# A hybrid mLSTM and attention block on one core: the later modulation sections summed on GpSimd during attention, and the inverse row sums spread by DMA

## The chip, the cores and the metric

The kernel runs on one core of a Trainium2 chip. A core has five engines with a queue of instructions each: TensorE (PE, matmuls; its weight loads are shown apart as PEld), VectorE (DVE), ScalarE (ACT), GpSimd (POOL) and SyncE (SP, which issues nearly all DMA transfers here). The metric is the device time of one launch in microseconds (us); less is better.

## The reference, cut to what matters

One layer of width 1024 on 1024 tokens with 256 tokens of context. A vector `c` gives six sections of 1024 numbers each, which shift, scale and gate the two halves of the layer:

```python
mod = (silu(c) @ w_mod + b_mod)                  # [1024] x [1024, 6*1024]
sh1, sc1, g1, sh2, sc2, g2 = split(mod, 6)
h = rmsnorm(x, norm1_g) * (1 + sc1) + sh1        # the context likewise, from c_ctx
y = token_mix(h, hc, ...)                        # input projections, mLSTM, attention, w_pa, w_pb, w_o
x = x + g1 * y
x = x + g2 * swiglu(rmsnorm(x, norm2_g) * (1 + sc2) + sh2, w_ffn_gate, w_ffn_up, w_ffn_down)
return rmsnorm(x, final_g)
```

Attention has 8 heads of width 128 with 2 key/value heads, over the 1024 tokens and the 256 of the context. Sections 0 and 1 are needed before the first projection. Section 2 (g1) is needed when `w_o` is loaded, which is scaled by it; sections 3 and 4 with the second norm; section 5 (g2) at the down projection.

## The kernel before, in words

Everything is in 32-bit floats. A product is made of three matmuls (`mm3`, L104 to L106) of operands split into a high and a low part (`split`, L98 on ACT and L99 on GpSimd or DVE). The stages follow one another: input projections in units of `w_in` (to about 800 us), mLSTM heads (to 1050), the merge of the mLSTM's halves, attention (about 1079 to 1393), a loop over eight column blocks n of `w_pb` (to 1506), a loop over `w_o` (to 1600), gate and up projections (to 2070) and the down projection. The Tile framework takes the program in the order in which it is written, sets the waits, and moves instructions within each engine's queue; an engine runs its queue strictly in order, so a waiting instruction holds all that stand behind it.

**Modulation.** `modulation_rest` computes half a section (512 columns) at each call and is called eight times: behind units 14 and 15 of the `w_in` loop, behind n = 1, 2, 4 and 5 of the `w_pb` loop, and behind u = 1 and 2 of the `w_o` loop. These are called places 0 to 7 below. A place loads four pieces of `w_mod` of 512 KB on SP (L293), runs 8 matmuls over them into one bank of PSUM (L300; the profile has 16 records for them), copies the bank to SBUF on DVE (L304), and then runs either one matmul that sums the four partial rows (L344, for the gates of sections 2 and 5) or four matmuls that also turn the row into a column (L312, for sections 3 and 4). L344 and L312 wait for the copy L304, and stand in PE's queue between the projection's matmuls.

**Attention** runs 64 steps (2 groups of heads, 8 blocks of 128 tokens, 4 heads). Four steps make a block; blocks are numbered 0 to 15 here. A step computes scores (L104 to L106 into `sc`), maxima (L1033), exponentials on ACT (L1043), the sum and its reciprocal (L1044, L1045), which DVE puts into a column of a tile `dg`, the transposes (L1054) and their split (L1057, L1058). `dg` is cleared by GpSimd ahead of each block (L1100). `attn_values` then multiplies by the values, for all four heads of the block before, in four parts spread over the next block's steps. In part 1 PE transposes `dg` (L1071), DVE copies the result (L1073), and GpSimd spreads the four rows of inverse sums over the 128 partitions with four `partition_broadcast`s (L1076) into `rs`. Behind part 3 DVE multiplies by `rs` (L1080). The next block's tokens are loaded by SP as `qr` (L1016). SP's queue during attention holds these loads and a few of keys, values and weights.

Of the kernel before, what the change touches and what calls it, by code (L numbers as in the profile page):

```python
# [9 lines left out]
F32 = mybir.dt.float32  # L10
F32R = mybir.dt.float32r
AF = mybir.ActivationFunctionType
ALU = mybir.AluOpType
# [4 lines left out]
P = 128  # L18
D = 1024
KT = D // P  # L20
S = 1024
CT = 256
NT = S // P
# [64 lines left out]
class Block:  # L88
# [241 lines left out]
                    nc.vector.tensor_tensor(t, v, bm[:, 8 + k:10 + k], op=ALU.add)  # L330
                    nc.vector.scalar_tensor_tensor(out=self.A1[:, s, k:k + 2], in0=t, scalar=1.0, in1=g1[:, k:k + 2], op0=ALU.add, op1=ALU.mult)

    def modulation_rest(self, ps, i):

        nc = self.nc
        bm = self.ch("b_mod")
        j0, b = (2, 5, 3, 4)[i // 2], i % 2
        c0 = j0 * D + b * 512
        rows = self.mod_block(ps, "X", (c0, c0 + 256))
        if i < 4:  # L340
            row = self.slots.get([P, 1024], F32)
            nc.sync.dma_start(row[0:1, 0:512], self.io["b_mod"][0:1, c0:c0 + 512])
            o = ps("Y", "mg")
            nc.tensor.matmul(o[0:2, :], lhsT=self.sel, rhs=rows[:, 0], start=True, stop=True)  # L344
            nc.vector.tensor_tensor(row[0:1, 512:1024], o[0:1, :], row[0:1, 0:512], op=ALU.add)
            nc.sync.dma_start(self.d_g[i // 2:i // 2 + 1, b * 512:(b + 1) * 512], row[0:1, 512:1024])
            self.slots.put(rows, row)
            return
        m = self.mod_channels(rows, ps, "Y", 1)[:, :, 0]
        hs = slice(4 * b, 4 * b + 4)  # L350
        if j0 == 3:
            nc.vector.tensor_tensor(self.B2[:, hs], m, bm[:, 24 + 4 * b:28 + 4 * b], op=ALU.add)
        else:
            t = self.st.tile([P, 4], F32, name="modt2", tag="modt2", bufs=2)
            nc.vector.tensor_tensor(t, m, bm[:, 32 + 4 * b:36 + 4 * b], op=ALU.add)
            nc.vector.scalar_tensor_tensor(out=self.A2[:, hs], in0=t, scalar=1.0, in1=self.ch("norm2_g")[:, hs], op0=ALU.add, op1=ALU.mult)


    def first_loads(self):
# [700 lines left out]
    def attn_values(self, pool, ps, g, t, PT, vv, dg, ya, part):  # L1060

        nc = self.nc
        if part == 0:
            self.av = ps("Z", "av")
        av = self.av
        for s in ((0, 1, 2), (3, 4), (5, 6, 7), (8, 9))[part]:
            pt = PT[s // 4]
            self.mm3(av, (vv[0][:, s], vv[1][:, s]), (pt[0][:, s % 4], pt[1][:, s % 4]), s == 0, s == NP - 1)
        if part == 1:
            rb = ps("Y", "pt")  # L1070
            nc.tensor.transpose(rb[:, 0:P], dg, self.idf)  # L1071
            rows = pool.tile([P, P], F32, name="rrow", tag="rrow", bufs=1)
            nc.vector.tensor_copy(rows, rb[:, 0:P])  # L1073
            self.rs = pool.tile([P, 512], F32, name="rs", tag="rs", bufs=1)
            for h in range(4):
                nc.gpsimd.partition_broadcast(self.rs[:, h * P:(h + 1) * P], rows[32 * h:32 * h + 1, :])  # L1076
        if part < 3:
            return
        rs = self.rs
        nc.vector.tensor_tensor(ya[:, 4 * g:4 * g + 4, t * P:(t + 1) * P], av.rearrange("p (h t) -> p h t", h=4),  # L1080
                                rs.rearrange("p (h t) -> p h t", h=4), op=ALU.mult)

    def attention(self, pool, ps):


        nc = self.nc
        kv, qs, dgs = {}, {}, {}
        kv[0] = self.attn_group_kv(pool, ps, 0)
        qs[0, 0] = self.attn_q(pool, ps, 0, 0)
        steps = [(g, t, h) for g in range(2) for t in range(NT) for h in range(4)]  # L1090

        def scores(i):
            if i >= len(steps):
                return None
            g, t, h = steps[i]
# [12 lines left out]
        yield  # L1108
        pr = scores(0)()
        ptp, ya = yield  # L1110
        PT, pend = None, None
        for i, (g, t, h) in enumerate(steps):
            if g == 0 and t == NT - 2 and h == 0:
                kv[1] = self.attn_group_kv(pool, ps, 1)
            if h and pend:
                self.attn_values(*pend, h)
            nxt = scores(i + 1)
            if h == 0:
                if pend:
                    self.attn_values(*pend, h)  # L1120
                PT = new_pt()
            self.attn_transpose(ps, h, pr, PT)
            if h == 1 and i + 3 < len(steps):
                qs[steps[i + 3][:2]] = self.attn_q(pool, ps, *steps[i + 3][:2])
            if h == 3:
                pend = (pool, ps, g, t, PT, kv[g][1], dgs[g, t], ya)
            pr = nxt() if nxt else None
        for part in range(4):
            self.attn_values(*pend, part)
        yield  # L1130


    def run(self):
        nc, tc, io = self.nc, self.tc, self.io
# [8 lines left out]
        def scratch(name, shape):  # L1143
            return dr.tile(shape, F32, name=name)
# [12 lines left out]
        self.d_mm = scratch("d_mm", [D, S])  # L1157
        self.d_ms = scratch("d_ms", [D, S])
        self.d_x1 = scratch("d_x1", [S, D])
        self.d_act = scratch("d_act", [FT // 2, 7, P, 512])  # L1160

        self.const, close_const = pool("const")
# [87 lines left out]
        X, later = {}, []  # L1250
# [5 lines left out]
        for i, u in enumerate(units):  # L1256
# [20 lines left out]
                more()  # L1277
            if i == 13:
                slots.put(*[t for p in self.cT for t in p])
            if i in (14, 15):  # L1280
                self.modulation_rest(PS, i - 14)
            if i == 22:
                while later:
                    more()
# [63 lines left out]

        pt, close_pt = pool("pt")
        w_pb = [self.load_s(slots, io["w_pb"], 0, KT, n * P, P) for n in range(2)]  # L1350
        attn.send((pt, yaf))
        close_pt()
        close_pa()

# [22 lines left out]
        for n in range(KT):  # L1377
# [15 lines left out]
                self.split(hi[:, n % 2], lo[:, n % 2], t[:, 0])  # L1393
                slots.put(t)
            slots.put(*w)
            if n in (1, 2, 4, 5):
                self.modulation_rest(PS, 3 + n if n < 3 else 2 + n)
            if n == KT - 2:
                load_o(0)
        for half in range(2):  # L1400
# [84 lines left out]
        for i, (half, u) in enumerate(units):  # L1485
# [22 lines left out]
                    r0 = (4 * half + t) * P  # L1508
                    nc.sync.dma_start(self.d_x1[r0:r0 + P, :], x1[t])
            slots.put(*w[0], *w[1])  # L1510
            if not half and u in (1, 2):
                self.modulation_rest(PS, 1 + u)
            if half and u == 2:
                for v in us:
                    self.t_own(v)
# [329 lines left out]
```

## Time and profile before

| | |
|---|---|
| runs of the kernel | 2314.78, 2306.33, 2312.02 us; median 2312.02 |
| the profiled execution | 2319.12 us (its span 2317.3) |
| mean granted TensorE clock | 0.975 |
| PE busy, of the span | 2173.9 us, 94% |
| DVE busy | 1588.6 us, 69% |
| ACT busy | 996.3 us, 43% |
| POOL busy | 767.0 us, 33% |
| DMA, mean rate | 113 GB/s |

Instruction rows of the timeline give a start, a duration, the line and operation, and in brackets the idle time ahead of the instruction with what ended it. Matmuls overlap: the pace of the projections is read from the starts, 0.23 us from one matmul of 512 columns to the next and 0.12 us for 256 columns. The granted clock is a share of full speed: 1.00 is the 2.4 GHz level and 0.50 the 1.2 GHz level.

### The profile page before, as it was taken

The numbers are of one execution on the slowest core, as the hardware profiler recorded it, in microseconds if no ns is written. First come the engines' busy times: TensorE is split into PE (matmuls) and PEld (weight loads), VectorE is DVE, ScalarE is ACT, GpSimd is POOL, SyncE is SP. The second block draws the span as 40 slices with busy tenths as digits, with TensorE's granted clock in tenths as the row PEclk, the third lists the DMA queues.
The fourth block names the chain that finished last, engine by engine and source line by source line (L and its number), as shares of the span: only waits on it lengthen the run. The fifth ranks groups of instructions, "written<-read, shape, count | busy, mean of one in ns | idle before, by whom it ended". The sixth has DMA issues, their size and how long they took to land. (4 is left out here: it accounts for less than half of the span.)

```text
span 2317.3 us, 31157 instructions
## 1 busy us (share of the span) xinstructions
PE 2173.9 (94%) x11387; PEld 1798.3 (78%) x11387; DVE 1588.6 (69%) x2855; ACT 996.3 (43%) x1997; POOL 767.0 (33%) x619
## 2 busy tenths in 40 slices
PE   5899999999999698999999998999899999998997
PEld 2698888977888587877888886789688888876875
DVE  4767576576878786876888873365746464678997
ACT  4424435243443564643777672134523232334332
POOL 1322222312323141311001004331564545457765
PEclk8999999999999899999999999999899999999999
DMA  7132323243232913036000016661132323264421
GB/s 259 55 92 89 103 92 105 83 150 128 70 113 98 310 58 114 13 130 234 15 21 21 15 42 203 220 225 71 46 128 91 118 93 113 97 219 177 159 91 73
DMA packets 179577, 262.43 MB, mean 113 GB/s; under 512 B 13136, under 2 KB 119640, under 8 KB 179424
## 3 DMA queue, kind: packets, MB, share of 16 engines
q1 hardware_dynamic: 169504, 236.62, 30.9%
q10 hardware_dynamic: 9920, 23.82, 2.6%
q8 instruction: 90, 1.47, 0.3%
q14 instruction: 63, 0.52, 0.1%
HBM read 190.10 MB, written 70.30 MB: 112 GB/s over the span
## 5 line engine op out<-in xcount | busy, mean ns | idle before, releaser
L98 ACT ACTIVATE s<-s 128x1024 fp32r<-128x1024 f32 (+2 forms) x446 | 369.5, 851 | 677.4 <-DVE s L233 79.1
L104 PE MATMUL pr<-s,s 128*128 128x512 f32 (+1 forms) x1736 | 624.3, 361 | 19.3 <-DVE s L261 9.9
L106 PE MATMUL pr<-s,s 128*128 128x512 f32 (+1 forms) x1736 | 622.8, 360 | 7.8 <-POOL s L99 4.8
L105 PE MATMUL pr<-s,s 128*128 128x512 f32 (+1 forms) x1736 | 623.4, 360 | 6.9 <-POOL s L99 4.9
L99 POOL TENSOR_TENSOR s<-s,s 128x1024 fp32r<-128x1024 f32 (+1 forms) x199 | 407.9, 2060 | 664.5 <-ACT s L98 455.3
L99 DVE TENSOR_TENSOR s<-s,s 128x1024 fp32r<-128x1024 f32 (+2 forms) x247 | 311.9, 1270 | 128.9 <-ACT s L98 105.5
L104 PEld LDWEIGHTS pr<-s,s 128*128 128x128 f32 x1736 | 331.4, 191 | 76.8 <-ACT s L98 13.1
L106 PEld LDWEIGHTS pr<-s,s 128*128 128x128 f32 x1736 | 330.8, 191 | 62.5 <-POOL s L99 7.0
L105 PEld LDWEIGHTS pr<-s,s 128*128 128x128 f32 x1736 | 331.0, 191 | 57.1 <-POOL s L99 6.0
L104 PE MATMUL pj<-s,s 128*128 128x512 f32 (+1 forms) x696 | 250.9, 361 | 18.1 <-DVE s L1743 13.5
L105 PE MATMUL pj<-s,s 128*128 128x512 f32 (+1 forms) x696 | 247.7, 356 | 7.3 <-POOL s L99 7.3
L106 PE MATMUL pj<-s,s 128*128 128x512 f32 (+1 forms) x696 | 247.5, 356 | 2.3 <-POOL s L99 2.3
L261 DVE TENSOR_TENSOR s<-s,pr 128x512 f32<-128x512 f32 x200 | 133.1, 681 | 84.3 <-PE pr L106 80.0
L1533 DVE TENSOR_TENSOR s<-s,pr 128x512 f32<-128x512 f32 x154 | 100.2, 680 | 114.8 <-ACT s L1549 78.5
L104 PEld LDWEIGHTS pj<-s,s 128*128 128x128 f32 x696 | 133.3, 192 | 50.8 <-DVE s L1743 20.1
L105 PEld LDWEIGHTS pj<-s,s 128*128 128x128 f32 x696 | 133.5, 192 | 25.8 <-POOL s L99 7.7
L106 PEld LDWEIGHTS pj<-s,s 128*128 128x128 f32 x696 | 133.2, 191 | 23.3 <-POOL s L99 3.0
L1058 DVE TENSOR_TENSOR PT<-pt,PT 128x512 fp32r<-128x512 f32 (+1 forms) x192 | 112.5, 598 | 35.3 <-ACT PT L1057 33.1
L1043 ACT ACTIVATE pr<-sc,st 128x512 f32<-128x512 f32 (+1 forms) x192 | 118.2, 623 | 34.4 <-DVE st L1035 33.9
L1543 POOL TENSOR_TENSOR s<-s,s 128x512 f32<-128x512 f32 x44 | 70.3, 1598 | 168.3 <-ACT s L98 71.6
L1057 ACT ACTIVATE PT<-pt 128x512 fp32r<-128x512 f32 (+1 forms) x192 | 94.6, 525 | 55.9 <-PE pt L1054 55.6
L1033 DVE TENSOR_REDUCE st<-sc 128x1 f32<-128x512 f32 (+1 forms) x192 | 109.6, 591 | 0.8 <-PE sc L106 0.8
(313 smaller groups left out, 3528.0 us busy)
## 6 DMA issues: line engine op xcount, KB each, us to landing
s<-in_w_in_dram SPq DMA_DIRECT2D x60, 512.0 KB, 3.7
d_act<-s SPq DMA_DIRECT2D x74, 256.0 KB, 2.1
s<-d_act SPq DMA_DIRECT2D x37, 512.0 KB, 5.3
s<-in_w_mod_dram SPq DMA_DIRECT2D x32, 512.0 KB, 6.1
s<-in_w_ffn_gate_dram SPq DMA_DIRECT2D x22, 512.0 KB, 4.5
s<-in_w_ffn_up_dram SPq DMA_DIRECT2D x22, 512.0 KB, 3.9
s<-in_w_ffn_down_dram SPq DMA_DIRECT2D x22, 512.0 KB, 5.1
s<-in_w_mod_dram SPq DMA_DIRECT2D x32, 256.0 KB, 4.5
```

What stands on the lines that cost most here:

```text
L98: nc.scalar.activation(hi, src, AF.Copy)
L99: (lo_eng or nc.gpsimd).tensor_tensor(lo, src, hi.bitcast(F32), op=ALU.subtract)
L104: nc.tensor.matmul(out, lhsT=lhs[0], rhs=rhs[0], start=first, stop=False)
L105: nc.tensor.matmul(out, lhsT=lhs[0], rhs=rhs[1], start=False, stop=False)
L106: nc.tensor.matmul(out, lhsT=lhs[1], rhs=rhs[0], start=False, stop=last)
L261: eng.tensor_tensor(out, a, b, op=ALU.add)
L1033: nc.vector.tensor_reduce(st[:, j:j + 1], o[:, 0:n], axis=AX.X, op=ALU.max)
L1043: nc.scalar.activation(pr[:, s0:s0 + n], sc[j][:, 0:n], AF.Exp, bias=st[:, 3:4], accum_out=st[:, 4 + j:5 + j])
L1057: nc.scalar.activation(hi, src, AF.Copy)
L1058: nc.vector.tensor_tensor(lo, src, hi.bitcast(F32), op=ALU.subtract)
L1533: nc.vector.tensor_tensor(out, a, b, op=ALU.add)
L1543: nc.gpsimd.tensor_tensor(g, g, o, op=ALU.mult)
```

## The change

`modulation_rest` is now a generator, which attention advances 36 times over its 64 steps: 32 of the advances each take one tile of `w_mod` (128 x 1024, 512 KB, two buffers `wm`, L347 on SP), multiply it on GpSimd by the 128 values of `silu(c)` that belong to its partitions (L362), and add it into an accumulator (L363). Eight such steps make a section. An accumulator is cleared by GpSimd (L352) and takes the row of `b_mod` into its first partition (L353). The other four advances end the sections: two matmuls with a tile of ones (L370), copies (L371) and a store (L372) for sections 2 and 5, or eight matmuls (L376) and one DVE operation for 3 and 4. The eight calls at the places above are gone. In `attn_values` the transpose of `dg` moves from part 1 to part 0, and the four broadcasts become two DMAs on SP: a store of the four rows to DRAM (`d_rs`, L1102) and a load that spreads them over the partitions (`rs`, L1103).

```diff
-    def modulation_rest(self, ps, i):
-        j0, b = (2, 5, 3, 4)[i // 2], i % 2
-        c0 = j0 * D + b * 512
-        rows = self.mod_block(ps, "X", (c0, c0 + 256))
...
+    def modulation_rest(self, pool):
+        nc, slots, ps = self.nc, self.slots, self.ps
+        sections = (2, 3, 4, 5)
+        seq = [(j0, k) for j0 in sections for k in range(KT)]
+        loaded, accs = [], {}
+        def load():
...
+            w = pool.tile([P, D], F32, name="wm", tag="wm", bufs=2)
+            nc.sync.dma_start(w, self.io["w_mod"][k * P:(k + 1) * P, j0 * D:(j0 + 1) * D])
+        def start(j0):
+            accs[j0] = slots.get([P, D], F32)
+            nc.gpsimd.memset(accs[j0], 0.0)
+            nc.sync.dma_start(accs[j0][0:1, :], self.io["b_mod"][0:1, j0 * D:(j0 + 1) * D])
...
+        for i, (j0, k) in enumerate(seq):
+            load()
+            if k == 2 and j0 != sections[-1]:
+                start(j0 + 1)
+            nc.gpsimd.tensor_scalar(loaded[i], loaded[i], self.sc[:, k, 0:1], None, op0=ALU.mult)
+            nc.gpsimd.tensor_tensor(acc, acc, loaded[i], op=ALU.add)
+            yield
+            if k + 1 < KT:
+                continue
+            if j0 in (2, 5):
+                for b in range(2):
+                    o = ps("Y", "mg")
+                    nc.tensor.matmul(o[0:2, :], lhsT=self.ones[:, 0:2], rhs=acc[:, b * 512:(b + 1) * 512], start=True, stop=True)
+                    nc.vector.tensor_copy(acc[0:1, b * 512:(b + 1) * 512], o[0:1, :])
+                nc.sync.dma_start(self.d_g[j0 // 5:j0 // 5 + 1, :], acc[0:1, :])
+            else:
+                m = ps("Y", "mch")
+                for j in range(KT):
+                    nc.tensor.matmul(m[:, j:j + 1], lhsT=acc[:, j * P:(j + 1) * P], rhs=self.ones[:, 0:1], start=True, stop=True)
...
-        if part == 1:
+        if part == 0:
             rb = ps("Y", "pt")
             nc.tensor.transpose(rb[:, 0:P], dg, self.idf)
-            rows = pool.tile([P, P], F32, name="rrow", tag="rrow", bufs=1)
+            rows = pool.tile([P, P], F32, name="rrow", tag="rrow", bufs=2)
             nc.vector.tensor_copy(rows, rb[:, 0:P])
             self.rs = pool.tile([P, 512], F32, name="rs", tag="rs", bufs=1)
-            for h in range(4):
-                nc.gpsimd.partition_broadcast(self.rs[:, h * P:(h + 1) * P], rows[32 * h:32 * h + 1, :])
+            i = g * NT + t
+            nc.sync.dma_start(self.d_rs[i], rows[0:P:32, :])
+            nc.sync.dma_start(self.rs, self.d_rs[i:i + 1].rearrange("o h t -> o (h t)").partition_broadcast(P))
...
+            if (i + 1) * 9 // 16 > i * 9 // 16:
+                next(side, None)
```

Where the scheduler puts the new work is read from the order of the queues. In SP's queue before, the loads of attention's first half follow one another with nothing between them; a last entry x6 stands for six rows alike.

```order
L1000 DMA vr<-d_v 128x2x128
L879 DMA d_ms<-s_9673 128x1024
L129 DMA s_9718<-in_w_pb_dram 128x8x128
L1016 DMA qr<-d_q 128x512 x6
L998 DMA kr<-d_k 128x2x128 x3
```

SP's queue in the change, from the store for block 0 to the loads for block 2 (a row ends with x2 or x4 where that many alike follow each other):

```order
L1102 DMA d_rs<-rrow 4x128
L347 DMA wm<-in_w_mod_dram 128x1024
L1103 DMA rs<-d_rs 128x512
L347 DMA wm<-in_w_mod_dram 128x1024 x2
L1042 DMA qr<-d_q 128x512
L347 DMA wm<-in_w_mod_dram 128x1024 x4
L1102 DMA d_rs<-rrow 4x128
L347 DMA wm<-in_w_mod_dram 128x1024
L1103 DMA rs<-d_rs 128x512
L347 DMA wm<-in_w_mod_dram 128x1024 x2
L1042 DMA qr<-d_q 128x512
L347 DMA wm<-in_w_mod_dram 128x1024 x2
```

Thirteen of the 32 `wm` loads now stand ahead of block 1's store, one more between that store and its load, and 18 in all ahead of block 2's store. From the third on, each `wm` load also waits for GpSimd's step two before it, which frees its buffer.

GpSimd's queue before, over attention's first blocks, behind two splits of weights (the rows named ISA are the broadcasts and what goes with them):

```order
L99 TENSOR_TENSOR s_9714<-s_9712,s_9713 128x1024
L99 TENSOR_TENSOR s_9720<-s_9718,s_9719 128x1024
L1100 MEMSET dg 128x128
L1076 ISA
L1076 ISA rs<-rrow 128x128 x4
L1100 MEMSET dg 128x128
L1076 ISA rs<-rrow 128x128 x4
```

The same queue in the change from the first of these splits on, with the waits in brackets (`s_9779` and `s_10004` are the accumulators of sections 2 and 3):

```order
L99 TENSOR_TENSOR s_9665<-s_9663,s_9664 128x1024 [waits DMAHW0_49,DVE_49,DMAHW4_49,PE_49,Activation_49]
L352 MEMSET s_9779 128x1024 [waits DMAHW5_49,DMAHW6_49,DMAHW1_49,Pool_49]
L362 TENSOR_SCALAR wm<-wm,sc 128x1024 [waits DMAHW3_49,DMAHW1_49]
L362 TENSOR_SCALAR wm<-wm,sc 128x1024 [waits DMAHW7_49,DMAHW4_49]
L363 TENSOR_TENSOR s_9779<-s_9779,wm 128x1024 [waits DMAHW6_49,Pool_49]
L363 TENSOR_TENSOR s_9779<-s_9779,wm 128x1024 [waits Pool_49]
L99 TENSOR_TENSOR s_9671<-s_9669,s_9670 128x1024 [waits DMAHW0_49,PE_49,Activation_49]
L352 MEMSET s_10004 128x1024 [waits DMAHW5_49,DVE_49,Pool_49]
L362 TENSOR_SCALAR wm<-wm,sc 128x1024 [waits DMAHW3_49]
L363 TENSOR_TENSOR s_9779<-s_9779,wm 128x1024 [waits Pool_49]
L362 TENSOR_SCALAR wm<-wm,sc 128x1024 [waits DMAHW5_49]
L363 TENSOR_TENSOR s_9779<-s_9779,wm 128x1024 [waits Pool_49]
```

The broadcasts are gone. Two multiplications and two additions, the first two steps, now stand between the two splits with a clearing ahead of them; behind the second split and another clearing a multiplication and an addition alternate, each multiplication behind the DMA of its tile, and the clearings of `dg` come between them.

## Rows read from the trace of the kernel before

**Rows 1.** The page: PE's busy time, share and instructions.

```profile
PE 2173.9 (94%) x11387; PEld 1798.3 (78%) x11387; DVE 1588.6 (69%) x2855; ACT 996.3 (43%) x1997; POOL 767.0 (33%) x619
```

**Rows 2.** Busy times in attention: window, length, engines (records), clock, DMA share, GB/s.

```profile
1079.00:1393.00 314.00, 309.29 (x1781) 255.19 (x1779) 249.95 (x628) 224.46 (x610) 31.59 (x85) 0.99 0.09 28
```

**Rows 3.** All instructions of lines L1073 and L1080: durations min/median/max, first and last start.

```profile
L1073 DVE COPY rrow<-pt x16: 271/292/293, 1103.8 to 1388.6; 128x128 f32<-128x128 f32 x16
...
L1080 DVE TENSOR_TENSOR yaf<-av,rs x16: 684/692/694, 1113.4 to 1392.2; 128x512 f32<-128x512 f32 x16
```

**Rows 4.** PE in the eight places: window, length, busy (records), clock, DMA share, GB/s.

```profile
510.50:522.80 12.30, 8.97 (x31) 0.86 0.76 277
538.34:545.45 7.11, 7.11 (x31) 1.00 0.26 76
1422.36:1426.42 4.06, 4.06 (x30) 1.00 0.85 278
1436.30:1440.56 4.26, 4.26 (x30) 1.00 0.54 145
1461.39:1465.45 4.06, 4.06 (x30) 1.00 0.00 0
1475.33:1487.63 12.30, 8.64 (x42) 0.87 0.56 191
1529.84:1538.76 8.92, 6.09 (x33) 0.82 0.78 289
1548.57:1554.10 5.53, 5.18 (x37) 1.00 0.77 239
```

**Rows 5.** Timeline of PE in places 0 and 5, stalls and the matmuls behind.

```profile
514.28 1.25 PE L300 MATMUL macc<-s,sc 128*32 128x512 f32 x8 [3.33 <-DMA s<-in_w_mod_dram]
...
1482.89 1.05 PE L312 MATMUL mch<-sel,s 128*128 128x1 f32 x8 [3.66 <-DVE s L304]
...
1484.70 0.63 PE L104 MATMUL pj<-s,s 128*128 128x512 f32 x1
1485.13 0.63 PE L105 MATMUL pj<-s,s 128*128 128x512 f32 x1
```

**Rows 6.** Timeline of PE in places 1 and 2: the closing matmuls.

```profile
544.56 1.02 PE L344 MATMUL mg<-s,sel 128*2 128x512 f32 x2
...
1425.62 1.00 PE L312 MATMUL mch<-sel,s 128*128 128x1 f32 x8
```

**Rows 7.** Waits in attention: engine, line, releaser; us in total, times, longest.

```profile
POOL dg L1100 <- PE pt L1071: 210.9, 14, 21.4
```

**Rows 8.** POOL's groups in attention and one of the mLSTM: busy, mean ns, idle before.

```profile
L1076 POOL PARTITION_BROADCAST rs<-rrow x64 | 20.3, 426 | 46.0 <-DVE rrow L1073 34.0 <-issue 11.5 <-DVE st L1035 0.6
L99 POOL TENSOR_TENSOR s<-s,s 128x1024 fp32r<-128x1024 f32 x2 | 4.7, 2372 | 41.3 <-DMA d_ms<-s 34.9 <-ACT s L98 6.3
...
L783 POOL MEMSET C<- 128x516 f32 x8 | 4.1, 528 | 10.3 <-PE pr L106 5.6 <-PE num L807 4.8
```

**Rows 9.** DMA issues: from and to, queue, count, KB each, median us to landing.

```profile
s<-in_w_pa_dram SPq DMA_DIRECT2D x8, 512.0 KB, 3.6
...
s<-d_sm SPq DMA_DIRECT2D x16, 256.0 KB, 2.9
...
kr<-d_k SPq DMA_DIRECT2D x10, 128.0 KB, 2.1
```

**Rows 10.** Timelines of POOL at attention's start, and of SP's issues in the `w_pb` loop.

```profile
1083.48 2.36 POOL L99 TENSOR_TENSOR s<-s,s 128x1024 fp32r<-128x1024 f32 x1 [34.93 <-DMA d_ms<-s]
...
1404.76 0.43 SPq L1385 DMA_DIRECT2D s<-d_ms  x1
```

**Rows 11.** Timeline of DVE for block 1: the copy of the inverse sums, and their use.

```profile
1123.13 0.29 DVE L1073 COPY rrow<-pt 128x128 f32<-128x128 f32 x1
...
1132.41 0.69 DVE L1080 TENSOR_TENSOR yaf<-av,rs 128x512 f32<-128x512 f32 x1 [0.18 <-PE av L106]
```

**Rows 12.** All instructions of L1533, which run beside GpSimd's additions.

```profile
L1533 DVE TENSOR_TENSOR s<-s,pr x154: 671/680/689, 1624.2 to 2076.2; 128x512 f32<-128x512 f32 x154
```

More of the change, by code (lines that the diff above doesn't have):

```diff
@@ L331, in modulation_first @@
                     nc.vector.scalar_tensor_tensor(out=self.A1[:, s, k:k + 2], in0=t, scalar=1.0, in1=g1[:, k:k + 2], op0=ALU.add, op1=ALU.mult)
-    def modulation_rest(self, ps, i):
-        nc = self.nc
-        bm = self.ch("b_mod")
-        j0, b = (2, 5, 3, 4)[i // 2], i % 2
-        c0 = j0 * D + b * 512
-        rows = self.mod_block(ps, "X", (c0, c0 + 256))
[L340 to L356, printed above, removed]
@@ new lines, in modulation_rest @@
+    def modulation_rest(self, pool):
[4 more added lines that the diff above has]
+        def load():
+            i = len(loaded)
+            if i >= len(seq):
+                return
+            j0, k = seq[i]
+            w = pool.tile([P, D], F32, name="wm", tag="wm", bufs=2)
+            nc.sync.dma_start(w, self.io["w_mod"][k * P:(k + 1) * P, j0 * D:(j0 + 1) * D])
+            loaded.append(w)
+        def start(j0):
+            accs[j0] = slots.get([P, D], F32)
+            nc.gpsimd.memset(accs[j0], 0.0)
+            nc.sync.dma_start(accs[j0][0:1, :], self.io["b_mod"][0:1, j0 * D:(j0 + 1) * D])
+        start(sections[0])
+        load()
+        for i, (j0, k) in enumerate(seq):
+            load()
+            if k == 2 and j0 != sections[-1]:
+                start(j0 + 1)
+            acc = accs[j0]
+            nc.gpsimd.tensor_scalar(loaded[i], loaded[i], self.sc[:, k, 0:1], None, op0=ALU.mult)
[13 more added lines that the diff above has]
+                    nc.tensor.matmul(m[:, j:j + 1], lhsT=acc[:, j * P:(j + 1) * P], rhs=self.ones[:, 0:1], start=True, stop=True)
+                if j0 == 3:
+                    nc.vector.tensor_copy(self.B2, m[:, 0:KT])
+                else:
+                    nc.vector.scalar_tensor_tensor(out=self.A2, in0=m[:, 0:KT], scalar=1.0, in1=self.ch("norm2_g")[:, 0:KT], op0=ALU.add, op1=ALU.mult)
+            slots.put(accs.pop(j0))
+            yield
@@ L1109, in attention @@
         pr = scores(0)()
-        ptp, ya = yield
+        ptp, ya, side = yield
         PT, pend = None, None
@@ L1159, in run @@
         self.d_x1 = scratch("d_x1", [S, D])
+        self.d_rs = scratch("d_rs", [2 * NT, 4, P])
         self.d_act = scratch("d_act", [FT // 2, 7, P, 512])
@@ L1279, in run @@
                 slots.put(*[t for p in self.cT for t in p])
-            if i in (14, 15):
-                self.modulation_rest(PS, i - 14)
             if i == 22:
@@ L1350, in run @@
         w_pb = [self.load_s(slots, io["w_pb"], 0, KT, n * P, P) for n in range(2)]
-        attn.send((pt, yaf))
+        wm, close_wm = pool("wm")
+        attn.send((pt, yaf, self.modulation_rest(wm)))
+        close_wm()
         close_pt()
@@ L1395, in run @@
             slots.put(*w)
-            if n in (1, 2, 4, 5):
-                self.modulation_rest(PS, 3 + n if n < 3 else 2 + n)
             if n == KT - 2:
@@ L1510, in run @@
             slots.put(*w[0], *w[1])
-            if not half and u in (1, 2):
-                self.modulation_rest(PS, 1 + u)
             if half and u == 2:
```

## The prediction, made before the change was run

> **What bounds the kernel now.** The page's list of engines comes first: PE is busy for 94% of the span, and no other engine comes near [rows 1]. So what counts is time that PE loses or is given. In attention, where the new work goes, the busy times by window have PE at 309.3 of 314 us, DVE at 250, ACT at 224, POOL at 31.6, with the DMA engines at 0.09 [rows 2]. The list of waits shows POOL there mostly waiting for PE ahead of the clearing of `dg`: 210.9 us in 14 waits [rows 7]. A block takes 18.6 us, the time from the first to the last use of `rs` over its 15 intervals [rows 3]. POOL and DMA have room, and PE has none. The reader is to see in the windows of the eight modulation places how much longer PE takes there than its matmuls need [rows 4].
>
> **What is removed.** Each window runs from just before one projection matmul to just before another, so that it holds whole paces. Its count of records holds 18 of the modulation where the gate's matmul ends it and 24 where a column's does, and one record (two at 256 columns) that reaches in from the left; the rest are projection matmuls. Places 0 to 7 so hold 12, 12, 5, 5, 5, 17, 13 and 17 or 18 of them; the first six at a pace of 0.23 us, the last two at 0.12 (the column of counts gives the 17; the starts give 18, and I take that). What is left of the lengths is 12.30 - 2.76 = 9.5, 7.11 - 2.76 = 4.3, 4.06 - 1.15 = 2.9, 4.26 - 1.15 = 3.1, 2.9, 12.30 - 3.91 = 8.4, 8.92 - 1.56 = 7.4 and 5.53 - 2.16 = 3.4: together **42.0 us** [rows 4]. All of it lies on PE's path. The undisturbed places cost about 3; the three dear ones (0, 5, 6) also hold a wait for the weights or for the copy of the rows, 3.33 and 3.66 us in two of them, and behind it matmuls 0.43 us apart where the pace is 0.23: the granted clock fell to the 1.2 GHz level after the idle time, the windows' mean being 0.86, 0.87 and 0.82 [rows 4, 5]. The places' 16 MB of weight loads leave stretches with DMA shares up to 0.85 [rows 4]; I count nothing for that.
>
> The 64 broadcasts take 20.3 us of POOL [rows 8] and two of them a further 11.5 us of issue, but they lie in POOL's idle time. Their removal gives nothing while `rs` was in time, as it was: for block 1 the copy ran at 1123.13 and the use at 1132.41, and that waited only 0.18 us, for PE [rows 11].
>
> **What is added on PE.** Four matmuls with ones cost as much as the pair of records of the gate's, 1.02 us each, 4.1 in all; eight column matmuls twice are twice the records of place 2's closing set, 2.0 each, 4.0 in all [rows 6]. That makes **+8.1**. They take banks of PSUM that the transposes use in turn, in six places; between nothing and one 0.68 us DVE operation for each [rows 12] I take **+2** (0 to 4). The moved transpose of `dg` costs nothing: it is the same transpose, one part earlier.
>
> **What is added on POOL and SP.** An addition takes 2.37 us [rows 8]. The multiplication by one value a partition is not in the trace. It reads one tensor and writes one, so the nearest row below it is a clearing that writes one, 0.528 us for 516 columns or 1.05 for 1024; above it is the two-input addition, 2.37 [rows 8]. I take 1.1, since it reads one stream as the addition does not, and keep both ends. A step is then 3.47 us. Loads as large landed in 3.6 us in the merge [rows 9]; with the DMA share at 0.09 in attention [rows 2] I take that. With two buffers, a tile is loaded again when its step ends: 3.6 + 3.47 and 0.2 for hand-over make 7.3 us for two steps, **3.65 a step**. The 32 steps need about 117 of the 314 us; POOL is never short of time as a whole.
>
> The Trainium skill ("GPSIMD Engine Reference", section 3.1) puts an operation of one or two arithmetic steps on GpSimd at 1.03 cycles per element; at the 1.2 GHz it counts with, an estimate from it is 0.88 us for 1024 columns. No run here shows that yet; the sum below would be 2 us lower by it.
>
> But the two queues are strict. `wm` loads wait for POOL, and the stores and loads of the row sums stand behind them on SP. For block 1: POOL's first split starts at 1083.48 [rows 10] and ends at 1085.8; a clearing, two multiplications and two additions (1.05 + 2.2 + 4.74) lead to 1093.8, the second split and a clearing to 1097.2, so step 3 ends at 1100.7 and step 12 at 1100.7 + 9 x 3.65 = 1133.6. The fourteenth `wm` load waits for that step, and the load of `rs` for block 1 stands behind it. At 0.43 us an issue [rows 10] it leaves at 1134.1, and at 2.9 us for 256 KB [rows 9] it lands at 1137.0. DVE wants it at 1132.41 [rows 11]: **4.6 late**. Block 0's comes in time: three loads fewer stand ahead of it. Block 2's store stands behind four more loads, at 1134.1 + 3 x 3.65 = 1145; PE itself was moved by 4.6 by then, so its due time of about 1156 holds. After this the queue has caught up: a block's 18.6 us hold five steps and more, while only two or three stand between stores. The same walk through the second half gives 1.2 late at the second group's values, whose splits on POOL stand among the last steps, and 1.2 behind the last block, where 3.6 us lie between copy and use [rows 3] and a store and a load (2.1 and 2.9 us) do not fit quite, although the copy comes earlier. Together **+7**; with the multiplication at 0.95 and loads in 3.3 it is 3.6, with 1.5 it is 12.5, with 1.75 it is 18. PE may lose the full clock after the first stall, as in place 5: seven intervals of 0.2 and an idle start, **+2**.
>
> **The sum** on the profiled execution's 2319.1 (2317.3 of span and 1.8 around it): -42.0 + 8.1 + 2 + 7 + 2 = -22.9, 2296.2. The profiled execution stands 7.1 above the median of the runs, so the forecast is **2289 us**. Its own range: 2275 where no queue is late, no bank waits and the loops gain a little from fewer loads, 2300 where the multiplication takes 1.75 and the lateness is 18.
>
> **Rivals.**
> (a) *The multiplication costs as much as the addition.* At 2.37 a step is 4.7 us, a block holds under four of them, and lateness grows: block 0's `rs` is 4 late, block 1's a further 20 with a clearing of `dg` stuck on POOL, block 4's 3, the second group's values 9, the end 1; 37 in all. Then -42.0 + 8.1 + 2 + 37 + 2 = +7, **2319**, slower than before. It decides where the lateness reaches 30, from a step of about 4.5 us; at a step of 4.1 (18 late) the change is still ahead. For it: every POOL row with a tensor as input is a two-input one. Against it: those rows read twice as much. Chance 0.11.
> (b) *GpSimd keeps DVE out.* If every step shut DVE off from its memory, DVE would need its 250 us beside 112 us of steps, 362 in a stretch of 314 [rows 2]: 48 more, of which all lands on PE: 2319.1 - 34 + 48 - 7 = **2326**, slower. DVE has 64 us of slack and the rest of the change gives 34, so it decides from 98 of the 112 us blocked. Against it: DVE operations with one input in PSUM and one in SBUF, attention's kind, take 671 to 689 ns beside POOL's additions [rows 12]; none is stretched. Chance 0.04.
> The Trainium skill ("SBUF — State Buffer", section "Who interferes with whom") says that a DVE instruction with at most one SBUF input, outside its two-port modes, does not contend with GpSimd; the row agrees with its 671 to 689 ns.
> (c) *No queue is late*, because the scheduler's steps run ahead of those I counted or loads land faster: -42.0 + 8.1 = -34, **2278**. Chance 0.15.
> (d) *The places' waits come back elsewhere*: what PE no longer waits for in places 0, 5 and 6 (some 10 us of stalls and 6 of half clock) it then waits for on the projection's own loads and splits. -22.9 + 16, **2305**. For it: the DMA share of 0.56 to 0.78 there; against it: much of that is the modulation's own loads [rows 4]. Chance 0.10.
>
> **How the numbers follow.** My forecast has 0.60, the rivals 0.11, 0.04, 0.15 and 0.10. The predicted time is the forecast's. The range, 2273 to 2313, takes in (c), (d) and the forecast with its bounds, and leaves out (a) and (b). A measurement here can tell 0.5% from no change, 11.6 us: faster means below 2300.5. The forecast gives 0.58 to faster and 0.02 to same; (c) is faster; (d) gives 0.02 to faster and 0.08 to same; (a) gives 0.08 to same and 0.03 to slower; (b) is slower. Together 0.75, 0.18 and 0.07.
>
> **What would show it.** Right: in the changed kernel's timeline no gap of PE in the `w_pb` and `w_o` loops that names a modulation line, those stages and the two units shorter by 42 together; POOL's multiplication near 1.1 us and steps near 3.65; one visible wait of DVE's multiplication by `rs` (for a DMA) in block 1, near 5 us, and attention longer by about 19 us than 314. Wrong: a multiplication above 2 us; waits for `rs` in many blocks; DVE operations longer than their medians before; or gaps of PE in the same loops that now name weights.

## The result and the profile after

The changed kernel takes **2336.97 us** (median of 4 runs, 2336.02 to 2338.47), the kernel before 2311.38 (4 runs, 2306.33 to 2314.78): a ratio of **1.0114, interval 1.0099 to 1.0129**. It is slower by 1.1%, where 2289 was forecast. The profiled execution took 2338.47 us (span 2336.7), 19.4 more than that of before.

The page's list of engines for the changed kernel, to be set beside [rows 1]. PE does less work (2159.8 against 2173.9 us) in a longer span; POOL does 147 us more.

```profile
PE 2159.8 (92%) x11259; PEld 1802.7 (77%) x11259; DVE 1590.9 (68%) x2843; ACT 994.1 (43%) x1995; POOL 914.0 (39%) x623
```

Three points of the program mark the stages: the first and the last use of `rs` (L1107, before L1080) and the last product of the `w_pb` loop (L1420, before L1390). The views of these lines, the first two of the changed kernel and the third of the one before; each row has the first and the last start behind the durations:

```profile
L1107 DVE TENSOR_TENSOR yaf<-av,rs x16: 691/692/692, 1102.9 to 1439.6; 128x512 f32<-128x512 f32 x16
L1420 DVE TENSOR_TENSOR s<-pj,s x16: 678/686/692, 1448.9 to 1543.6; 128x512 f32<-128x512 f32 x16
```

```profile
L1390 DVE TENSOR_TENSOR s<-pj,s x16: 678/692/693, 1407.0 to 1508.7; 128x512 f32<-128x512 f32 x16
```

With [rows 3] the stages are: up to the first use 1113.4 before and 1102.9 now (**-10.5**); from the first to the last use 278.8 and 336.7 (**+57.9**); from there to the end of the `w_pb` loop 116.5 and 104.0 (**-12.5**); the rest of the span 808.6 and 793.1 (**-15.5**). Together +19.4. The stage up to the first use also holds the first harm, a wait of 5.9 us of that first use for its `rs`:

```profile
1102.95 0.69 DVE L1107 TENSOR_TENSOR yaf<-av,rs 128x512 f32<-128x512 f32 x1 [5.94 <-DMA rs<-d_rs]
```

With it counted whole to attention, attention took 63.8 us and the places gave 44.4. That is profile against profile, and the profiled execution of before stands 7.7 us above the median of its runs, that of the change 1.5 above. By the medians (+25.6) the places gave some 38, if attention is alike in every execution.

POOL's groups in the changed attention (busy, mean ns of one, idle before), to be set beside [rows 8]:

```profile
L362 POOL TENSOR_SCALAR wm<-wm,sc 128x1024 f32<-128x1024 f32 x32 | 91.1, 2846 | 7.9 <-DMA wm<-in_w_mod_dram 7.9
L363 POOL TENSOR_TENSOR s<-s,wm 128x1024 f32<-128x1024 f32 x32 | 76.1, 2378 | 5.6 <-DMA s<-in_b_mod_dram 3.3
```

The multiplication takes **2.85 us**, more than the addition, where 1.1 was put into the sum. A step is 5.25 us. What that does to block 1 is seen in SP's queue, in DVE's timeline and in PE's, in this order:

```profile
1119.58 10.88 SPq L347 DMA_DIRECT2D wm<-in_w_mod_dram  x3
1130.56 0.51 SPq L1102 DMA_DIRECT2D d_rs<-rrow  x1
1135.38 0.33 SPq L347 DMA_DIRECT2D wm<-in_w_mod_dram  x1
1135.80 0.38 SPq L1103 DMA_DIRECT2D rs<-d_rs  x1
```

```profile
1139.99 0.69 DVE L1107 TENSOR_TENSOR yaf<-av,rs 128x512 f32<-128x512 f32 x1 [16.57 <-DMA rs<-d_rs]
```

```profile
1125.07 0.60 PE L1080 MATMUL pt<-idf,pr 128*128 128x128 f32 x4
1141.16 1.08 PE L1080 MATMUL pt<-idf,pr 128*128 128x128 f32 x4 [15.49 <-DVE PT L1084]
1141.90 0.78 PE L104 MATMUL sc<-kT,qt 128*128 128x512 f32 x1
1142.47 0.63 PE L105 MATMUL sc<-kT,qt 128*128 128x512 f32 x1
1142.90 0.63 PE L106 MATMUL sc<-kT,qt 128*128 128x512 f32 x1
```

The store follows the thirteenth `wm` load, and the load of `rs` the fourteenth; both stand behind POOL's steps. (A row with x3 merges three issues and the waits between them.) DVE waits 16.6 us at the head of its queue. Behind it stands the split of the transposes (L1084), which frees the banks of PSUM that PE's next transposes want, so PE stands still for 15.5 us. Behind the gap its matmuls run 0.43 us apart in place of 0.23, the 1.2 GHz level, as in place 5 of the kernel before [rows 5]; the granted clock there is 0.50:

```profile
1141.20:1145.00 3.80, 3.80 (x12) 3.14 (x13) 3.32 (x9) 1.54 (x4) 3.72 (x2) 0.50 0.46 138
```

The windows of the changed attention show it by stage (PE, PEld, DVE, ACT and POOL busy, granted clock, DMA share, GB/s). In the first 200 us, which hold most of the steps, PE has gaps and a clock of 0.88 and 0.93; once the steps are done it is as in [rows 2].

```profile
1103.00:1200.00 97.00, 77.97 (x412) 62.45 (x413) 60.52 (x150) 50.76 (x138) 79.44 (x35) 0.88 0.32 101
1200.00:1300.00 100.00, 80.51 (x447) 65.91 (x445) 60.04 (x151) 53.50 (x146) 56.52 (x30) 0.93 0.28 84
1300.00:1440.00 140.00, 138.65 (x780) 113.34 (x781) 110.40 (x267) 96.19 (x260) 11.57 (x13) 0.99 0.09 28
```

The same windows from the first to the last use of `rs`, in the change, in the kernel before, and in the last kernel of the experiments below, which has the same work on PE and little of the lateness:

```profile
1102.90:1439.60 336.70, 296.73 (x1635) 241.35 (x1636) 230.62 (x567) 200.44 (x541) 147.62 (x76) 0.94 0.22 66
```

```profile
1113.40:1392.20 278.80, 278.08 (x1609) 230.42 (x1608) 222.13 (x561) 200.23 (x548) 25.35 (x78) 1.00 0.07 23
```

```profile
1094.20:1385.70 291.50, 288.01 (x1648) 234.87 (x1647) 233.46 (x571) 201.65 (x549) 136.61 (x104) 1.00 0.27 82
```

So the 57.9 us are 39 of gaps on PE (336.7 - 296.7, against 0.7 before), some 10 of added matmuls (288.0 against 278.1 at a clock of 1.00) and some 9 of lost clock (296.7 against 288.0).

The list of waits in the changed attention (1060 to 1440 us; the last two rows are the second group's values, in block 8):

```profile
DVE yaf L1107 <- DMA rs<-d_rs: 36.3, 5, 16.6
PE pt L1080 <- DVE PT L1084: 31.1, 7, 15.5
PEld av L106 <- POOL vv L99: 4.9, 1, 4.9
PE av L106 <- POOL vv L99: 4.5, 1, 4.5
```

### The profile page after: what moved, and what is told of

The parts are those of the page before. It is cut to its first block, busy times and chain, and to the rows that moved or that the text cites. A ratio compares the mean times of both kernels' runs of the same rounds, so it can differ in the third digit from the quotient of the medians.

```text
span 2336.7 us, 30919 instructions
## 1 busy us (share of the span) xinstructions
PE 2159.8 (92%) x11259; PEld 1802.7 (77%) x11259; DVE 1590.9 (68%) x2843; ACT 994.1 (43%) x1995; POOL 914.0 (39%) x623
## 5 line engine op out<-in xcount | busy, mean ns | idle before, releaser
L105 PEld LDWEIGHTS pj<-s,s 128*128 128x128 f32 x696 | 133.6, 192 | 19.3 <-DVE s L99 2.5
L1084 DVE TENSOR_TENSOR PT<-pt,PT 128x512 fp32r<-128x512 f32 (+1 forms) x192 | 112.9, 599 | 47.2 <-ACT PT L1083 45.5
L1080 PE MATMUL pt<-idf,pr 128*128 128x128 f32 x640 | 100.5, 283 | 31.9 <-DVE PT L1084 31.1
```

What stands on the lines that cost most here:

```text
L105: nc.tensor.matmul(out, lhsT=lhs[0], rhs=rhs[1], start=False, stop=False)
L1080: nc.tensor.transpose(tp[:, i * P:(i + 1) * P], pr[:, s0 + i * P:s0 + (i + 1) * P], self.idf)
L1084: nc.vector.tensor_tensor(lo, src, hi.bitcast(F32), op=ALU.subtract)
```

## The experiments

The theory after this: a step of 5.25 us, issued early in two in-order queues, keeps the row sums' store and load, the clearing of `dg` and the second group's values behind it, and PE pays with gaps and with its clock. The rivals: the way through DRAM is slow by itself; the places' gain is not real; GpSimd slows the other engines wherever its work falls. Each median below is set against runs of the kernel before that ran beside it (medians 2312 to 2314). The table has the time of one block, the distance between two uses of `rs` in the trace of each kernel (blocks 1 to 9, us). Kernels are named as in the headings below.

| kernel | 1 | 2 | 3 | 4 | 5 | 6 | 7 | 8 | 9 |
|---|---|---|---|---|---|---|---|---|---|
| before | 19.1 | 18.8 | 19.0 | 19.4 | 20.1 | 19.6 | 19.2 | 20.0 | 18.8 |
| the change | 37.0 | 23.6 | 21.3 | 25.9 | 25.6 | 19.3 | 20.9 | 33.3 | 19.3 |
| rs only | 19.3 | 19.3 | 19.3 | 19.2 | 20.0 | 19.4 | 19.3 | 20.3 | 19.3 |
| no multiplication | 23.6 | 20.0 | 21.5 | 19.2 | 20.1 | 19.3 | 20.9 | 24.4 | 19.4 |
| two-input multiplication | 30.3 | 20.5 | 21.5 | 22.3 | 23.8 | 19.3 | 21.0 | 28.5 | 19.3 |
| loads on GpSimd | 19.3 | 28.4 | 34.9 | 19.2 | 21.5 | 19.3 | 20.9 | 31.0 | 19.2 |
| modulation only | 25.9 | 26.2 | 25.9 | 25.9 | 37.9 | 21.3 | 27.5 | 44.6 | 16.7 |
| paced | 19.3 | 21.0 | 21.2 | 19.2 | 21.1 | 19.5 | 21.0 | 24.9 | 19.3 |
| paced, values on DVE | 19.3 | 22.8 | 22.4 | 19.3 | 21.0 | 19.5 | 20.9 | 19.1 | 19.0 |
| paced, values on DVE, two-input | 19.3 | 19.3 | 21.5 | 19.3 | 21.2 | 19.6 | 20.9 | 21.0 | 19.0 |

### rs only: the row sums by DMA, the modulation as before

```diff
-        if part == 1:
+        if part == 0:
...
-            for h in range(4):
-                nc.gpsimd.partition_broadcast(self.rs[:, h * P:(h + 1) * P], rows[32 * h:32 * h + 1, :])
+            i = g * NT + t
+            nc.sync.dma_start(self.d_rs[i], rows[0:P:32, :])
+            nc.sync.dma_start(self.rs, self.d_rs[i:i + 1].rearrange("o h t -> o (h t)").partition_broadcast(P))
```

> Modulation stays where it was before; only the row sums' inverse goes by DMA. Theory (GpSimd's 5.25 us steps hold SP's queue, and with it the stores and loads of rs): with no weight loads ahead of them on SP the store and the load land within the some 9 us that block 1 had, so the time is that of before, 2311 +- 6, and the wait of DVE's multiplication by rs for a DMA is under 3 us in all. Rival (the way through DRAM is late by itself): a wait in most of the 16 blocks, 2330 or more.

Measured: 2314.95 us, ratio 0.9999 (0.9986 to 1.0012). One wait for `rs`, behind the last block, from the list of waits:

```profile
DVE yaf L1081 <- DMA rs<-d_rs: 5.7, 1, 5.7
```

The wait is longer than the 3 us expected, and it falls where the walk had put 1.2. The blocks take 19.3, some 0.3 more than before, which these runs don't explain. But for the last block the way through DRAM is in time when SP is free; that rival falls.

### No modulation: sections 2 to 5 left out

```diff
-        rows = self.mod_block(ps, "X", (c0, c0 + 256))
...
+        nc.sync.dma_start(self.d_g[0:1, :], self.io["b_mod"][0:1, 2 * D:3 * D])
+        nc.sync.dma_start(self.d_g[1:2, :], self.io["b_mod"][0:1, 5 * D:6 * D])
+        nc.vector.tensor_copy(self.A2, self.ch("norm2_g")[:, 0:KT])
+        nc.vector.tensor_copy(self.B2, self.ch("b_mod")[:, 24:32])
```

> The kernel before with the sections 2 to 5 of the modulation left out (the gates are b_mod's rows alone, the norm's scale is norm2_g, its shift b_mod's part); attention as before. Theory (the places cost PE what their windows showed): 42 us less than before, 2269, 2263 to 2276. Rival (the waits of the places come back as waits for weights): 16 of it are lost, 2285 or more.

Measured: 2275.65 us, ratio 0.9836 (0.9816 to 0.9856), which is 38 us less than before (33 to 43). Attention is untouched: its uses of `rs` span 278.5 us, as before's 278.8 [rows 3].

```profile
L1064 DVE TENSOR_TENSOR yaf<-av,rs x16: 683/692/694, 1093.6 to 1372.1; 128x512 f32<-128x512 f32 x16
```

The 42.0 read from the windows of the places lies within this interval; the waits did not come back elsewhere, which would have left 26.

### No multiplication, and the two-input multiplication

Two kernels with shorter steps. The first leaves the multiplication out; the second keeps all work, and every row of SP's and of POOL's queue stands where it stood in the change. The edit of the second:

```diff
-            nc.gpsimd.tensor_scalar(loaded[i], loaded[i], self.sc[:, k, 0:1], None, op0=ALU.mult)
+            nc.gpsimd.tensor_tensor(loaded[i], loaded[i], self.sc[:, k, 0:1].to_broadcast([P, D]), op=ALU.mult)
```

> The change with GpSimd's multiplication left out (sections 2 to 5 are sums of w_mod alone); a step is then the addition, 2.4 us. Theory: the queues are late by 1 to 5 us in all in place of some 50, and the places' gain shows: 2311 - 42 + 8 + 2 + 3 = 2282, 2276 to 2292; DVE's wait for rs falls from 36 to under 8. Rival (the number of loads on SP ahead of the stores matters, not the length of a step): still 2310 or more, with waits for rs over 20.

Measured: 2292.24 us, ratio 0.9905 (0.9882 to 0.9929), at the upper edge of what was expected; the wait for `rs` is 8.4 us in two places, just over the 8 expected. Fifteen loads stand ahead of block 1's store here, thirteen in the change: the rival, that their number matters and not the length of a step, falls.

> The change with GpSimd's multiplication written as the two-input form with a repeated column (1.90 us in the run of forms, in place of 2.85); the same work and the same order in every queue, a step of 4.3 us in place of 5.25. Theory (lateness grows with the step by the walk through the queues): the walk gives 50 us of lateness at 2.85 and 22 at 1.90, so the time falls by 28 from 2337, to 2302 to 2316, and DVE's wait for rs in block 1 from 16.6 to about 10. Rival (what costs is that GpSimd works beside attention at all, or the way of rs): a fall by no more than GpSimd's own 2 or 3 us behind the last wait, 2330 or more.

Measured: 2312.24 us, ratio 0.9981 (0.9965 to 0.9996). The multiplication took 1.90, and the wait for `rs` in block 1 fell from 16.6 to 11.6. The views of POOL's groups and of the waits:

```profile
L362 POOL TENSOR_TENSOR wm<-wm,sc 128x1024 f32<-128x1024 f32 x32 | 60.6, 1896 | 9.6 <-DMA wm<-in_w_mod_dram 9.6
```

```profile
DVE yaf L1107 <- DMA rs<-d_rs: 19.6, 4, 11.6
```

0.95 us less in each of 32 steps, 30 us of GpSimd, took 25 us from the time by the medians, and 28 if each kernel is set against the kernel before that ran beside it. The walk through the queues gives 28. With the same order in both queues, a shorter step alone brings the time from 1.1% above the kernel before to 0.2% below it: the length of the step, in this order of the queues, is the cause.

### The multiplication's price, by form

```diff
-            nc.gpsimd.tensor_scalar(loaded[i], loaded[i], self.sc[:, k, 0:1], None, op0=ALU.mult)
+            x = loaded[i]
+            if j0 == 2:
+                nc.gpsimd.tensor_scalar(x, x, self.sc[:, k, 0:1], None, op0=ALU.mult)
+            elif j0 == 3:
+                nc.gpsimd.tensor_scalar(x, x, 0.5, None, op0=ALU.mult)
+            elif j0 == 4:
+                nc.gpsimd.tensor_tensor(x, x, self.sc[:, k, 0:1].to_broadcast([P, D]), op=ALU.mult)
+            else:
+                nc.gpsimd.tensor_scalar(x[:, 0:512], x[:, 0:512], self.sc[:, k, 0:1], None, op0=ALU.mult)
+                nc.gpsimd.tensor_copy(x[:, 512:1024], x[:, 0:512])
```

> What GpSimd's multiplication costs, by form; the change with the multiplication written in another way in each section (so sections 3 and 5 are not the reference's): section 2 as in the change, in section 3 by a constant in the instruction, in section 4 a two-input multiplication by a column repeated along the row, in section 5 the change's form on 512 columns and a copy of 512. Theory (the operation with a scalar has a dear loop of its own per element, whatever the scalar): 2.85 us in section 2, 2.8 to 2.9 in section 3, 1.4 to 1.5 for 512 columns, and the two-input form at its 2.4. Rival A (fetching a scalar for each partition is what costs): section 3 falls to 1.0 to 1.5. Rival B (a fixed cost at each instruction): the 512 columns cost over 1.8.

Measured (2321.72 us, one run; POOL's groups, shapes kept apart):

```profile
L364 POOL TENSOR_SCALAR wm<-wm,sc 128x1024 f32<-128x1024 f32 x8 | 22.8, 2850 | 0.0
L366 POOL TENSOR_SCALAR wm<-wm 128x1024 f32<-128x1024 f32 x8 | 22.2, 2772 | 0.0
L368 POOL TENSOR_TENSOR wm<-wm,sc 128x1024 f32<-128x1024 f32 x8 | 15.2, 1896 | 6.0 <-DMA wm<-in_w_mod_dram 6.0
L370 POOL TENSOR_SCALAR wm<-wm,sc 128x512 f32<-128x512 f32 x8 | 12.5, 1567 | 4.2 <-DMA wm<-in_w_mod_dram 4.2
...
L371 POOL COPY wm<-wm 128x512 f32<-128x512 f32 x8 | 4.9, 611 | 0.5
```

A constant in place of a scalar from each partition saves 0.08 us: fetching the scalar is not the cost. Half the columns cost 1.57, a little over the 1.4 to 1.5 expected; if the cost is linear, a column costs 2.5 ns ((2850 - 1567) / 512) and an instruction 0.28 us. A copy of 512 columns, which also reads one tensor and writes one, costs 0.61. So one stream in and one out is not what makes the price; it belongs to this operation. The two-input form was expected at 2.4 and came at 1.90: a repeated column is cheaper than a second full tensor (the addition's 2.38). Why, these rows don't tell.

### Loads on GpSimd's queue

```diff
-            nc.sync.dma_start(w, self.io["w_mod"][k * P:(k + 1) * P, j0 * D:(j0 + 1) * D])
+            nc.gpsimd.dma_start(w, self.io["w_mod"][k * P:(k + 1) * P, j0 * D:(j0 + 1) * D])
```

> The change with the weight loads issued by GpSimd in place of SP; GpSimd's steps are as many and as long, SP's queue holds none of them. Theory with SP's queue as the main harm: waits for rs go (36 to under 8), what stays is the clearing of dg and the second group's values behind steps on GpSimd, some 15 to 25 us of it, and the issue on GpSimd on top: 2295 to 2320. Rival (GpSimd's own queue is the main harm): 2325 or more.

Measured: 2318.83 us, ratio 1.0021 (1.0004 to 1.0039). The waits for `rs` go, but for 3.7 us, and block 1 is back at 19.3. In their place DVE waits for the clearing of `dg`, which now stands behind the same steps and the issues on POOL; blocks 2, 3 and 8 take 28, 35 and 31:

```profile
DVE dg L1071 <- POOL dg L1127: 20.1, 2, 12.9
```

Both queues do harm. Taking the loads off SP leaves the kernel 5 to 7 us above the one before, where the change is 26 above; the next late thing takes over.

### Modulation only: the broadcasts stay on GpSimd

```diff
-        if part == 0:
+        if part == 1:
...
-            i = g * NT + t
-            nc.sync.dma_start(self.d_rs[i], rows[0:P:32, :])
-            nc.sync.dma_start(self.rs, self.d_rs[i:i + 1].rearrange("o h t -> o (h t)").partition_broadcast(P))
+            for h in range(4):
+                nc.gpsimd.partition_broadcast(self.rs[:, h * P:(h + 1) * P], rows[32 * h:32 * h + 1, :])
```

> The modulation as in the change, the row sums spread by GpSimd's broadcasts as before (the other part undone). Each block then holds two steps (10.5 us), four broadcasts (1.7) and two changes between kinds of GpSimd work, of which one showed as 5.7 us of issue before: 18 to 24 us against a block of 18.6. Theory: GpSimd becomes the bound of the blocks that have steps, 2295 to 2350, and the issue time at the broadcasts grows from 11.5 to over 60 us. Rival (the change of kind is hidden): as the paced kernel, 2285 to 2295.

Measured: 2396.72 us, ratio 1.0358 (1.0326 to 1.039), outside the expected 2350. POOL's timeline over some 25 us has two of the changes of kind:

```profile
1203.35 0.21 POOL L1126 MEMSET dg<- 128x128 f32 x1
1210.45 1.29 POOL L1102 PARTITION_BROADCAST rs<-rrow  x4 [6.88 <-issue]
1218.59 5.69 POOL L362 TENSOR_SCALAR wm<-wm,sc 128x1024 f32<-128x1024 f32 x2 [6.85 <-issue]
1224.26 4.86 POOL L363 TENSOR_TENSOR s<-s,wm 128x1024 f32<-128x1024 f32 x2
```

The list of waits has 88.5 us of them ahead of broadcasts and 84.5 ahead of multiplications:

```profile
POOL rs L1102 <- issue: 88.5, 13, 7.6
POOL wm L362 <- issue: 84.5, 12, 7.6
```

Each way costs some 7 us (88.5 in 13 and 84.5 in 12). The expectation had taken the 5.7 of one way. So the two parts of the change belong together: alone, the row sums' part gives nothing, and the modulation's part costs 3.6%, against 1.1% of both; the DMA route keeps GpSimd at one kind of work.

### The multiplication on ACT

```diff
-            nc.gpsimd.tensor_scalar(loaded[i], loaded[i], self.sc[:, k, 0:1], None, op0=ALU.mult)
+            nc.scalar.activation(loaded[i], loaded[i], AF.Copy, scale=self.sc[:, k, 0:1])
```

> The change with the multiplication moved from GpSimd to ACT (some 0.85 us each, 27 in all, on an engine that is busy 224 of attention's 314 us); nothing is left out. Theory: as without the multiplication, 2276 to 2296, below both kernels. Rival (ACT, waiting in order for the weight's DMA, delays the exponentials): PE waits for ACT's rows, 2300 or more.

Measured: 2302.96 us, ratio 0.9947 (0.9931 to 0.9964), faster than both kernels but outside the expected range. ACT took 1.16 us for one and waited for the weights ahead of it:

```profile
L362 ACT ACTIVATE wm<-wm,sc 128x1024 f32<-128x1024 f32 x32 | 37.2, 1163 | 15.4 <-DMA wm<-in_w_mod_dram 15.1
```

Behind it on ACT stand the exponentials and ACT's part of the transposes' split, on the chain to PE. PE's waits for that split are more in number here than without the multiplication (the first row this kernel, the second the one without):

```profile
PE pt L1080 <- DVE PT L1084: 13.9, 15, 2.7
```

```profile
PE pt L1079 <- DVE PT L1083: 7.1, 4, 3.3
```

This speaks for the rival in part; it is not shown that ACT's waits cause all of the 11 us between the two kernels.

### Paced: all work of the change, spread

```diff
             w = pool.tile([P, D], F32, name="wm", tag="wm", bufs=2)
+            nc.gpsimd.tensor_copy(w[0:1, 0:1], self.pace[0:1, 3:4])
...
             sc, st = self.attn_scores(pool, ps, h, qs[g, t], kv[g][0])
+            self.pace = st
```

> The change with all its work and its 5.25 us steps, but each weight load waits (through a copy of one element on GpSimd) for the scores of the attention step at which it is written in the program, so that some two steps fall to a block in place of five. Theory (a long step does harm only because many steps stand ahead of the stores and of the clearing of dg on in-order queues): DVE's wait for rs falls from 36 to under 8 us and the time to 2280 to 2296, below before. Rival (GpSimd's 167 us of work slow the other engines wherever they fall): the sum of lost time stays, 2320 or more.

Measured: 2294.43 us, ratio 0.9911 (0.988 to 0.9941). The steps cost what they cost in the change, and the wait for `rs` is 4.3 us, once (POOL's timeline over one step, and the wait):

```profile
1172.13 2.85 POOL L363 TENSOR_SCALAR wm<-wm,sc 128x1024 f32<-128x1024 f32 x1 [3.90 <-DMA wm<-in_w_mod_dram]
1175.07 2.38 POOL L364 TENSOR_TENSOR s<-s,wm 128x1024 f32<-128x1024 f32 x1
1177.88 0.18 POOL L347 COPY wm<-st 1x1 f32<-1x1 f32 x1 [0.43 <-DVE st L1062]
```

```profile
DVE yaf L1108 <- DMA rs<-d_rs: 4.3, 1, 4.3
```

GpSimd's 167 us of steps do not slow the other engines by themselves; where they stand in the queues does. Nor is it the traffic of the weight loads, which is the same here: the DMA share from the first to the last use of `rs` is 0.27, and 0.22 in the change. This kernel is 43 us below the change by the medians.

> As the paced kernel, and the multiplication on ACT in place of GpSimd (ACT 1.15 us each as the earlier run showed, 37 us in all). Theory: GpSimd is free, but ACT lies nearer to PE's path: 2278 to 2300, about the paced kernel or a little above it. Rival (ACT's place in the chain of exponentials and transposes costs nothing when the loads come in time): clearly below the paced kernel, 2275 or less.

With the multiplication on ACT as well: 2295.51 us, ratio 0.9924 (0.9896 to 0.9953). No difference from the paced kernel can be told.

### Paced, with the values' split on DVE

```diff
-            self.split(vv[0][:, 2 * q:2 * q + 2], vv[1][:, 2 * q:2 * q + 2], vr)
+            self.split(vv[0][:, 2 * q:2 * q + 2], vv[1][:, 2 * q:2 * q + 2], vr, nc.vector)
```

> The paced kernel with the split of attention's values moved from GpSimd to DVE, since its block 8 still takes 24.9 us where the kernel before has 20.0, with the second group's splits behind steps on GpSimd. Theory: block 8 falls to some 20.5 and the time by 4, to 2287 to 2294. Rival (DVE's splits, which read two inputs from SBUF, wait for GpSimd's reads): block 8 stays at 23 or more and the time at 2290 to 2300.

Measured: 2286.09 us, ratio 0.9878 (0.9858 to 0.9898), a little below the expected range; block 8 takes 19.1, so the rival falls. Blocks 2 and 3 take 22.8 and 22.4, longer than in the paced kernel.

> The paced kernel with the values' split on DVE and the two-input multiplication. Theory (paced, GpSimd has room, so its step's length no longer matters): within 4 us of the kernel without it, 2282 to 2290. Rival (paced steps still hold something up, as blocks of 21 to 22.8 us may show): 2278 or less.

With the two-input multiplication as well: 2284.63 us, ratio 0.9871 (0.9852 to 0.989), 30 us below the kernel before it ran beside (2314.47) and the fastest that leaves no work out. The last step of it makes no difference that can be told: paced, GpSimd has room.

## Why the prediction was wrong, point by point

- **What bounds the kernel.** Right: PE, and what it loses or is given.
- **What is removed, 42.0.** Right within its uncertainty: 38 (33 to 43) alone; in the change 44 by the stages of the two profiles and some 38 by the medians.
- **PE's additions, 8.1 and 2.** In the last paced kernel blocks 3 and 7, which hold two gate matmuls and a set of columns, take 21.5 and 20.9 where most others take 19.3: 1.6 to 2.2 each, near the 2.0 forecast.
- **The multiplication, 1.1 us.** This step failed. The multiplication was put at the clearing's end of a range of 1.05 to 2.37, because it reads one tensor, and it took 2.85, above the upper end. The reason given (one stream is cheap, two are dear) does not hold: the two-input form takes 1.90, the one-input form 2.85. Nor was every POOL row with a tensor as input a two-input one, as rival (a) says: three selects of 128x128 (L151 and L152 are two of them) read one tensor and took 0.294 us, where clearing as many columns takes 0.205. The estimate of 0.88 from the Trainium skill ("GPSIMD Engine Reference", section 3.1) differs from the 2.85 too; the measurement decides.
- **The walk through the queues.** Right in its mechanism and its place: block 1, the store behind the thirteenth load and the load of `rs` behind the fourteenth. At 2.85 in place of 1.1 POOL's own steps set the pace, 5.22 us a step in place of 3.65; the same walk then has block 0's `rs` 6.3 us late and block 1's a further 17.6, and DVE waited 5.9 and 16.6. One reading in it is wrong: ahead of block 0's store stand seven loads fewer, not three, by the order of SP's queue; only with seven does that block come in time at 1.1. Nor has the queue caught up behind block 2: blocks 2 and 4 waited 3.0 and 6.7 us. In all the walk at 2.85 was put at 50 us after the result, where 7 was forecast; how the later blocks make up the 50 is not worked out on record, and PE's gaps grew by 39 between the first and the last use of `rs`.
- **The lost clock, 2.** Mis-sized too: one stall was foreseen, there were several, and the clock cost some 9 us. With 39 of gaps and 10 of added matmuls that makes the +57.9 of attention.
- **The block, 18.6 us.** The mean over 15 intervals takes in the last, which is 9.7 us long; the other 14 are 19.2. No term of the sum hangs on it.
- **The rivals.** (a) is what happened, with a price further out than the one it was given: it was sized at a multiplication of 2.37, 37 us late and 2319, and got 0.11. It decided, as said there, where the lateness passes 30; the two-input kernel, at a step of 4.3, sits just below that line, at the time of the kernel before. (b) is excluded: DVE's split of the transposes keeps its median of 681 ns beside the steps (L1084, and L1058 before), and the paced kernel keeps its gain. (d) is excluded by the kernel without modulation. (c), at 2278, is nearest to the paced kernels, but the change itself was late.
- **The range** ended at 2313. It left out (a) altogether, though the price on which (a) hung was in no row, and both ends of that price were taken from other operations.

The two views of the split of the transposes, the first in the changed kernel, the second before:

```profile
L1084 DVE TENSOR_TENSOR PT<-pt,PT x192: 415/681/693, 1066.3 to 1430.0; 128x512 fp32r<-128x512 f32 x128, 128x256 fp32r<-128x256 f32 x64
```

```profile
L1058 DVE TENSOR_TENSOR PT<-pt,PT x192: 414/681/694, 1083.9 to 1385.6; 128x512 fp32r<-128x512 f32 x128, 128x256 fp32r<-128x256 f32 x64
```

## What to carry to other kernels

Work that was moved to an idle engine was paid for here by what stood behind it in in-order queues: look where the scheduler puts it, and bind each piece to the step of the main work that it should keep pace with, here by one copied element, which turned 26 us slower into 18 faster. An operation that is not in the trace has no price until it has been run; a range between two other operations is none, and the forecast's sign should not hang on it. Undo each part of a change alone before judging it: here one part gave nothing alone, and the other did great harm without it.

## What was not expected of the hardware

- GpSimd's multiplication by one scalar takes 2.85 us for 128 x 1024 in 32-bit floats, 2.77 with a constant; the same product as a two-input multiplication with a repeated column takes 1.90, and a copy of 512 columns 0.61.
- A change between broadcasts and the multiplications on GpSimd cost some 7 us each way (5.9 to 7.6), with the engine idle, where the kernel before had shown 5.7 twice in attention, on the way to broadcasts.
